# TensorE's order in the expert stage written out, Pool's residual passes one behind each scatter, expert weights ten chunks ahead

## The chip, the cores and the metric

One of the eight cores of a Trainium2 chip runs the kernel. The metric is the device time of one execution in microseconds (us). A core has five instruction streams that run side by side and wait for each other by semaphores: TensorE (PE in the profile; PEld is its weight load), VectorE (DVE), ScalarE (ACT), GpSimd (POOL) and SyncE (SP), which here only starts DMAs. Each stream runs strictly in its own order.

## The reference

One step of a backbone with two layers, model width 1024, for 128 context and 256 latent tokens, all fp32. A layer is a token mixer and then a mixture of experts, each inside `x <- LayerNorm(ALPHA*x + gate*sublayer(x*(1+scale)+shift))`. The change lies in the experts:

```python
def hier_moe(h, rg_w, rg_b, re_w, re_b, w1, w3, w2):      # h: 384 tokens x 1024
    g_idx = jnp.argmax(t @ rg_w + rg_b, axis=-1)          # one of 4 groups
    e_sel = ...                                           # its 8 expert logits
    top_v, top_i = lax.top_k(e_sel, 2)                    # two of 8 experts
    top_w = jax.nn.softmax(top_v, axis=-1) * g_p
    gate = ...                                            # 384 x 32, two entries a row
    hid = silu(einsum('td,edf->tef', t, w1)) * einsum('td,edf->tef', t, w3)
    return einsum('tef,efd->td', hid * gate, w2)          # 32 experts, each 1024 -> 128 -> 1024
```

## The kernel before, in words

The first 400 us of a layer's 570 or so are the mixer, which the change does not touch. Then comes the expert stage (`experts`, L1290), which runs once a layer.

The 32 experts are taken as 8 quads of four. Every expert has 32 token slots, and two experts of each quad (`who`, found at run time) get a second block of 32. A token is brought to its slots by one-hot matmuls: `gather(J)` (L1308) makes `xT`, 256 columns, the slots of two quads (J = 0 to 3), or `xB`, the second blocks of four quads (J = 4, 5). It has four steps of 12 matmuls (L1319), each evacuated from a `tp` bank, of which there are two; its one-hot matrix `oh` comes from VectorE (L1282, L1283) and needs `sidj`. `gather0` (L1322) is the first one in a form of its own.

A quad q then has these pieces:

- up: four weight chunks of 1 MB. Of each, `up_first` (L1362) is 8 matmuls with the weights in place, `up_second` (L1372) 8 matmuls with the weights of the two experts that `who` names, copied out to `hv` first (two copies a chunk, two of three on VectorE at L1353, one of three on ScalarE; `hv` has two buffers).
- hidden: Silu on ScalarE, a product on VectorE (L1381, `hid`), transposes on TensorE (L1383, L1385), a copy on VectorE (L1388, `hidT`).
- down: 8 matmuls with the second weights (L1398), 8 more with copies of them (L1405), in two `sc` banks; ScalarE and VectorE evacuate them to `ys` (two buffers) and `ys2` (one buffer), and Pool scatters each to memory by an indirect DMA (L1410), 14 a layer before the last quad. The last quad's rows stay on the chip.

`slots` (L1239) places the scatters' addresses and gates. `affine` (L1502) finishes the residual `r` on Pool: for three row blocks a subtraction and scaling (L1506), a product with `lg` (L1508) and a sum with `lb` (L1509). Both loads of `g20` and `g21` (L1512) then reuse the memory of `lg` and `lb`. After the last quad's hidden, a branch (L1519) for tokens beyond 64 in an expert, not taken here, and then the scattered rows come back (`yy`, L1589) and are summed with the last quad's (L1496, L1498) for the second LayerNorm.

The weights come in one queue, SyncE's, in the order of the program: 32 up chunks (L328; six `raw` buffers and four `wx` buffers, four of every ten chunks in `wx`) and 16 loads of 1 MB for down (L338, w2, four buffers). `done` (L343) asks for the next chunk after each one used, six ahead (`NRAW`). The last four chunks are held behind the fourteenth w2 load (L326).

Each stream's order is worked out by a scheduler when the kernel is built, from what each instruction needs, except inside `manual_schedule`, where the stream keeps the program's order; `issue_after` puts an instruction behind a named one.

Of the kernel before, what the change touches and what calls it, by code (L numbers as in the profile page):

```python
# [14 lines left out]
ALU = mybir.AluOpType  # L15
# [7 lines left out]
NT = 3  # L23
# [3 lines left out]
NQUAD = 8  # L27
NHALF = 16
# [49 lines left out]
class Kern:  # L78
# [177 lines left out]


    NRAW = 6

    def start_stream(self):  # L260

        o = []
        for l in range(L):
            ada = [("a", l, g, kp) for g in (1, 2) for kp in range(4)]
            if l + 1 < L:
                ada += [("a", l + 1, 0, kp) for kp in range(4)]
            for n in range(NPIECE // 4):
                if l == 0 and n < 2:
                    o.append(("a", 0, 0, n))
                o.append(("w", l, n))  # L270
                if l == 0 and n == 1:
                    o += [("a", 0, 0, 2), ("a", 0, 0, 3)]
                if n >= 1 and ada:
                    o.append(ada.pop(0))
            o += [("e", l, j) for j in range(NHALF)]
        self.order = [(*k, h) for k in o for h in range(2)]
        self.pos = {k: i for i, k in enumerate(self.order)}
        self.loaded = {}
        self.nload = 0
        self.ndone = 0  # L280
        self.limit = self.pos["w", 1, 0, 0]
        self.last_load = None
        self.prepped = {}

    def first_dma(self, out, in_):
# [26 lines left out]
    def load_to(self, n):  # L312
        if self.first_loads:
            return
        while self.nload < min(n, self.limit):
            k = self.order[self.nload]
            if k[0] == "e" and k[2] % 5 >= 3:
                w = self.wx.tile([128, 2048], F32, tag="wx", name="w_x")
            else:
                w = self.rawp.tile([128, 2048], F32, tag="raw", name="w_raw")  # L320
            src = {"a": lambda: self.a["wada"][(k[1] * 3 + k[2]) * 4 + k[3], k[4]],
                   "w": lambda: self.a["wst"][k[1] * (NPIECE // 4) + k[2], k[3]],
                   "e": lambda: self.a["w13"][k[1] * NHALF + k[2], k[3]]}[k[0]]()
            if k[0] == "e" and k[2] >= NHALF - 2:
                with self.tc.issue_after(self.w2_ins[k[1], NHALF - 3].ins):
                    self.nc.sync.dma_start(w, src)  # L326
            else:
                self.last_load = self.nc.sync.dma_start(w, src)  # L328
            self.loaded[k] = w
            self.nload += 1  # L330

# [13 lines left out]
    def done(self):  # L345

        self.ndone += 1
        self.load_first()
        self.load_to(self.ndone + self.NRAW)

    def prep(self, l, n):
        if n >= NPIECE or (l, n) in self.prepped:
# [787 lines left out]
    def gates(self, lg):  # L1140
        nc, mo, pc, m8, e8 = self.nc, self.mo, self.pc, self.m8, self.e8
        S = lambda name, shape, dt=F32: mo.tile([128, *shape], dt, name=name)
        sid, N6 = self.sid, 2 * NT
        self.sidj = S("sidj", (8, N6))
        self.sidj_ins = nc.vector.scalar_tensor_tensor(self.sidj, self.con[:, C_I32:C_I32 + 8].unsqueeze(2).to_broadcast([128, 8, N6]),
                                       -256.0, sid.rearrange("p i c -> p (i c)").unsqueeze(1).to_broadcast([128, 8, N6]),
                                       op0=ALU.mult, op1=ALU.add)

        ex = S("ex", (NT, 6))
        nc.vector.tensor_tensor(ex[:, :, 0:4], lg[:, :, 0:4], m8[:, :, 0:1].to_broadcast([128, NT, 4]), op=ALU.subtract)  # L1150
        nc.vector.tensor_tensor(ex[:, :, 4:6], e8[:, :, 0:2], e8[:, :, 0:1].to_broadcast([128, NT, 2]), op=ALU.subtract)
        with self.tc.issue_after(self.evac_ins.ins):
            self.act(ex, ex, AF.Exp)
        self.act(S("dum", (1,)), ex[:, 0, 0:1], AF.Silu)
        se = S("se", (NT, 2))
        nc.vector.tensor_reduce(se[:, :, 0], ex[:, :, 0:4], axis=AX.X, op=ALU.add)
        nc.vector.tensor_reduce(se[:, :, 1], ex[:, :, 4:6], axis=AX.X, op=ALU.add)
        nc.vector.reciprocal(se, se)
        nc.vector.tensor_tensor(se[:, :, 0], se[:, :, 0], se[:, :, 1], op=ALU.mult)
        self.W = S("W", (NT, 2))  # L1160
        nc.vector.tensor_tensor(self.W, ex[:, :, 4:6], se[:, :, 0:1].to_broadcast([128, NT, 2]), op=ALU.mult)


    def second(self):
        nc, mo, V = self.nc, self.mo, self.nc.vector
        S = lambda name, shape, dt=F32: mo.tile([128, *shape], dt, name=name)
        N6 = 2 * NT
        cnt = self.pc[:, 96:128].rearrange("p (q e) -> p q e", e=4)
        full = S("full", (NQUAD, 4))
        V.tensor_scalar(full, cnt, float(CAP), None, op0=ALU.is_gt)  # L1170
# [119 lines left out]
    def experts(self, l):  # L1290
        nc, mo, ep, tc = self.nc, self.mo, self.ep, self.tc
        scat = []
        iota = self.con[:, C_I256:C_I256 + 256]
        ident4 = self.ident.rearrange("p (i z r) -> p i z r", i=2, z=2)
        engines = [nc.vector.engine, nc.scalar.engine]
# [12 lines left out]
        def gather(J):  # L1308

            oh = self.onehot(J)  # L1310
            xT = slot_rows(J)
            for z in range(4):
                ps = self.bank("tp")
                for d2 in range(2):
                    d = z * 2 + d2
                    n = 0
                    for i in range(NT):
                        for t in (self.thi, self.tlo):
                            nc.tensor.matmul(ps[:, d2 * 256:(d2 + 1) * 256], t[:, i, d * 128:(d + 1) * 128], oh[:, i, :],  # L1319
                                             start=n == 0, stop=n == 5)  # L1320
                            n += 1
                evac(xT, z, ps)  # L1322
            return xT

        def gather0(oh):

# [49 lines left out]
        def hidden(ps):  # L1376
# [2 lines left out]
            hid = ep.tile([128, 3, 64], F32, tag="hid", name="hid", bufs=1)  # L1379
            self.act(hid, pv[:, :, 0, :], AF.Silu)  # L1380
            nc.vector.tensor_tensor(hid, hid, pv[:, :, 1, :], op=ALU.mult)  # L1381
            pt = self.bank("ms")
            nc.tensor.transpose(pt[:, 0:128], hid[:, 0:2, :].rearrange("p h f -> p (h f)"), self.ident)  # L1383
            for h in range(2):
# [24 lines left out]
        def scatter(view, rows, dst, n):  # L1409
# [3 lines left out]
            for o in scat:  # L1413
                tc.declare_no_dep(ins.ins, o.ins, reason="rows of other slots")
            scat.append(ins)

        def down(q, hT, who):
            ys = ep.tile([128, D], F32, tag="ys", name="ys", bufs=2)
# [14 lines left out]
        def down_keep(q, hT, who):  # L1433
# [11 lines left out]
                self.lo_ins = nc.vector.scalar_tensor_tensor(lo, src, g, hi.bitcast(F32), op0=ALU.mult, op1=ALU.subtract)  # L1445
            return ys, y2

        self.load_w2(l, 3)
        xT = gather0(self.oh0)
        self.gates(self.logit)  # L1450
        with tc.issue_after(self.oh0_ins.ins):
            self.second()
        _, who = nc.values_load_multi_w_load_instructions(
            self.who[0:1].rearrange("p q i -> p (q i)"), engines=engines, min_val=0, max_val=3,
            skip_runtime_bounds_check_because="a place among four, worked out as one")
        who = [who[2 * q:2 * q + 2] for q in range(NQUAD)]
        self.slots()
        xB = gather(4)
        for q in range(NQUAD - 1):
            ps = self.bank("mm")  # L1460
            for kq in range(4):
                up_first(ps, q, kq, xT)
                up_second(ps, q, kq, xB, who[q])
            hT = hidden(ps)
            if q % 2 == 0:
                nx = gather(q // 2 + 1) if q < 6 else None
            else:
                xT = nx
            if q == 3:
                xB = gather(5)  # L1470
            down(q, hT, who[q])
            if q == 0:
                self.affine(l, scat[0])
        q = NQUAD - 1
        ps = self.bank("mm")
        for kq in range(4):
            up_first(ps, q, kq, xT)
            up_second(ps, q, kq, xB, who[q])
        hT = hidden(ps)
        self.overflow(l)  # L1480
        self.load_yy(l)

# [17 lines left out]

    def affine(self, l, scat):

        nc, a, md = self.nc, self.a, self.m_d[l]
        with self.tc.issue_after(scat.ins):
            for i in range(NT):
                nc.gpsimd.tensor_scalar(self.r[:, i, :], self.r[:, i, :], self.nmean[:, i:i + 1], self.rs1[:, i:i + 1],  # L1506
                                        op0=ALU.add, op1=ALU.mult)
                nc.gpsimd.tensor_tensor(self.r[:, i, :], self.r[:, i, :], self.rows["lg"], op=ALU.mult)  # L1508
                nc.gpsimd.tensor_tensor(self.r[:, i, :], self.r[:, i, :], self.rows["lb"], op=ALU.add)  # L1509
        for s in range(2):  # L1510
            t = self.mo.tile([128, D], F32, tag="row", name=f"g2{s}", bufs=2)
            nc.sync.dma_start(t, md[1, s:s + 1, 1024:2048].to_broadcast([128, D]))  # L1512
            self.rows[f"g2{s}"] = t


    def overflow(self, l):
# [368 lines left out]
```

## Time and profile before

| | us |
|---|---|
| median of 3 runs | 1181.82 (1181.38 to 1182.83) |
| the profiled execution | 1179.99 |
| its span, first to last instruction | 1178.2 |
| TensorE's busy time in it | 1050.0 (89%) |
| VectorE's busy time | 835.5 (71%) |
| Pool's busy time | 284.2 (24%) |
| mean granted TensorE clock | 0.946 |

The expert stage of layer 0 runs from about 425 to 600 us of the span, that of layer 1 from about 995 us to the end. A row of a timeline gives when an instruction (or several of one kind, xN) started, how long it took, and in brackets how long its engine stood idle before it and what released it. The granted clock is a share of full speed.

### The profile page before, as it was taken

The page shows a single profiled execution, that of the slowest core. Times are in us where ns is not written, and L with a number is a line of the kernel's source. Part 1 is how long each engine was busy: PE and PEld are TensorE (multiplying, and loading weights), DVE is VectorE, ACT ScalarE, POOL GpSimd, SP SyncE. Part 2 cuts the span into 40 slices and gives each one's busy share as a digit, 9 for nine tenths or more (in the row PEclk, how much of TensorE's full clock was granted, in tenths as well). Part 3 has the DMA queues.
Part 4 walks back from the last instruction along what each step waited for, and adds up shares of the span by engine and source line. Part 5 has one row for each costly group of instructions (what it writes and reads, how often), then busy time and mean ns, then how long its engine had stood idle before and what let it go on. Part 6 is the DMA issues. An engine that isn't in the chain of part 4 may idle for free. (4 is left out here: it accounts for less than half of the span.)

```text
span 1178.2 us, 21160 instructions
## 1 busy us (share of the span) xinstructions
PE 1050.0 (89%) x8446; PEld 881.1 (75%) x8446; DVE 835.5 (71%) x1542; ACT 401.5 (34%) x687; POOL 284.2 (24%) x238
## 2 busy tenths in 40 slices
PE   7999999999999859598789999999999996859864
PEld 5898968878999848365359897788899996636532
DVE  3389999964458794754379999987634778684537
ACT  3334344453334121132253334435433422212222
POOL 0002411321101530611244043123110054061015
PEclk8999989999999968798889999999999998879997
DMA  9967568357366544599595756772233675468964
GB/s 356 400 235 269 208 241 316 119 192 273 110 232 255 185 175 165 219 398 418 234 345 173 272 206 248 268 274 100 77 139 111 248 269 202 152 237 330 419 255 158
DMA packets 53950, 279.37 MB, mean 237 GB/s; under 512 B 7932, under 2 KB 12028, under 8 KB 26705
## 3 DMA queue, kind: packets, MB, share of 16 engines
q1 hardware_dynamic: 49344, 269.75, 60.4%
q0 software_dynamic: 4496, 8.14, 1.9%
q8 instruction: 71, 1.16, 0.4%
q14 instruction: 39, 0.31, 0.1%
HBM read 261.86 MB, written 21.56 MB: 241 GB/s over the span
## 5 line engine op out<-in xcount | busy, mean ns | idle before, releaser
L95 PE MATMUL ps_mm<-hThi,wr 128*128 128x384 f32 x672 | 230.3, 344 | 5.3 <-ACT hThi L100 2.9
L108 DVE TENSOR_TENSOR wr<-w_raw,wr 128x1024 fp32r<-128x1024 f32 x124 | 163.0, 1315 | 95.9 <-ACT wr L100 95.6
L97 PE MATMUL ps_mm<-hThi,wr 128*128 128x384 f32 x672 | 228.0, 339 | 1.3 <-DVE wr L108 1.3
L96 PE MATMUL ps_mm<-hTlo,wr 128*128 128x384 f32 x672 | 228.1, 339 | 0.4 <-DVE hTlo L437 0.2
L100 ACT ACTIVATE wr<-w_raw 128x1024 fp32r<-128x1024 f32 x140 | 147.3, 1055 | 68.7 <-PE ps_mm L97 36.4
L501 DVE SCALAR_TENSOR_TENSOR cacc<-pad,par,cacc 128x399 f32<-128x399 f32 x240 | 167.4, 698 | 4.1
L95 PEld LDWEIGHTS ps_mm<-hThi,wr 128*128 128x128 f32 x672 | 127.2, 189 | 21.8 <-ACT hThi L100 5.2
L97 PEld LDWEIGHTS ps_mm<-hThi,wr 128*128 128x128 f32 x672 | 127.3, 189 | 3.6 <-DVE wr L108 1.6
L96 PEld LDWEIGHTS ps_mm<-hTlo,wr 128*128 128x128 f32 x672 | 127.2, 189 | 2.8 <-DVE hTlo L437 1.3
L1410 POOL DMA_INDIRECT y_d<-ys,dst x28 | 28.5, 1019 | 238.3 <-ACT hv L100 89.5
L1372 PE MATMUL ps_mm<-hv,xB 128*32 128x128 f32 x1024 | 51.1, 280 | 29.3 <-DVE hv L1353 28.7
L108 POOL TENSOR_TENSOR wr<-w_raw,wr 128x1024 fp32r<-128x1024 f32 x10 | 24.8, 2478 | 207.8 <-ACT wr L100 207.3
L1372 PEld LDWEIGHTS ps_mm<-hv,xB 128*32 128x32 f32 x1024 | 36.3, 111 | 42.7 <-DVE hv L1353 35.7
L1319 PE MATMUL ps_tp<-oh,thi 128*128 128x256 f32 x240 | 66.7, 311 | 1.6 <-DVE xB L1302 1.6
L1319 PE MATMUL ps_tp<-oh,tlo 128*128 128x256 f32 x240 | 64.0, 300 | 0.0
L1353 DVE COPY hv<-w_x 128x512 f32 x36 | 47.6, 1367 | 17.4 <-PE ps_mm L1372 9.9
L1319 PEld LDWEIGHTS ps_tp<-oh,thi 128*128 128x128 f32 x240 | 50.0, 209 | 11.3 <-issue 4.9
L1319 PEld LDWEIGHTS ps_tp<-oh,tlo 128*128 128x128 f32 x240 | 49.9, 208 | 1.2 <-issue 1.0
L1398 PE MATMUL ps_sc<-w,hidT 128*32 128x512 f32 x256 | 36.2, 670 | 16.2 <-PEq L1519 8.4
L100 ACT ACTIVATE gate<-ps_mm 128x384 f32<-128x384 f32 x40 | 19.7, 491 | 85.7 <-PE ps_mm L97 84.7
L211 PE MATMUL ps_ms<-w_raw,cT 128*32 128x512 f32 x320 | 47.3, 621 | 0.0
L1362 PE MATMUL ps_mm<-w_raw,xT 128*32 128x256 f32 x640 | 47.1, 385 | 0.0
(491 smaller groups left out, 2383.0 us busy)
## 6 DMA issues: line engine op xcount, KB each, us to landing
w_raw<-in_wst SPq DMA_DIRECT2D x68, 1024.0 KB, 6.5
w_raw<-in_wada SPq DMA_DIRECT2D x48, 1024.0 KB, 5.2
w_raw<-in_w SPq DMA_DIRECT2D x40, 1024.0 KB, 9.0
w<-in_w SPq DMA_DIRECT2D x32, 1024.0 KB, 10.3
w_x<-in_w SPq DMA_DIRECT2D x24, 1024.0 KB, 9.4
bias<-in_bias SPq DMA_DIRECT2D x8, 768.0 KB, 8.7
y_d<-zero SPq DMA_DIRECT2D x2, 3072.0 KB, 15.7
yy<-y_d SPq DMA_DIRECT2D x6, 1024.0 KB, 8.1
```

Source lines behind the costliest of these rows:

```text
L95: mm(out, whi, xhi, start=first, stop=False)
L96: mm(out, whi, xlo, start=False, stop=False)
L97: mm(out, wlo, xhi, start=False, stop=last)
L100: return self.nc.scalar.activation(out, in_, f, **k)
L108: (eng or self.nc.vector).tensor_tensor(lo, x, hi.bitcast(F32), op=ALU.subtract)
L211: nc.tensor.matmul(ps[32 * t:32 * t + 32, :], self.cT[:, 2 * kp + k, :], w[:, t * 512:t * 512 + 512], start=(kp == 0 and k == 0), stop=(kp ...
L501: nc.vector.scalar_tensor_tensor(acc, pad[:, j:j + W], w, acc, op0=ALU.mult, op1=ALU.add)
L1319: nc.tensor.matmul(ps[:, d2 * 256:(d2 + 1) * 256], t[:, i, d * 128:(d + 1) * 128], oh[:, i, :], start=n == 0, stop=n == 5)
L1353: nc.vector.tensor_copy(hv[:, i, :], src)
L1362: nc.tensor.matmul(ps[e * 32:(e + 1) * 32, 0:256], xT[:, k, c:c + 32], w[:, e, kk, :], start=k == 0, stop=k == 7, skip_group_check=True)
L1372: nc.tensor.matmul(ps[t * 32:(t + 1) * 32, 256:384], xB[:, k, c:c + 32], hv[:, i, kk, h * 128:(h + 1) * 128], start=False, stop=k == 7, sk ...
L1398: nc.tensor.matmul(po[e * 32:(e + 1) * 32, :], hT[:, e * 32:(e + 1) * 32], w2[:, e, :], start=True, stop=True)
```

## The change

Three things, all in the expert stage.

The order of TensorE's instructions there is that of the program. The program now gives: `gather0`, then `up_first` of quads 0 and 1 (64 matmuls), `gather(4)`, `up_second` and hidden of quad 0, `slots`; then for each quad the up, the down of the quad before it, the transposes of hidden (`hidden_T`), and half of a gather. `sidj` is made in `second` with the columns that are used, four and two.

`affine` is a generator that is advanced by each scatter: one Pool pass behind each of the first nine. The two loads that reuse the memory of `lg` and `lb` come in the program with the tenth scatter.

`done` asks for chunks ten ahead in this stage, and the first ten are asked for at its start; the four last chunks are no longer held behind a w2 load.

```diff
+    ahead = NRAW
...
-            if k[0] == "e" and k[2] >= NHALF - 2:
-                with self.tc.issue_after(self.w2_ins[k[1], NHALF - 3].ins):
-                    self.nc.sync.dma_start(w, src)
-            else:
-                self.last_load = self.nc.sync.dma_start(w, src)
+            self.nc.sync.dma_start(w, src)
...
-        self.load_to(self.ndone + self.NRAW)
+        self.load_to(self.ndone + self.ahead)
...
+            next(aff, None)
...
-        xB = gather(4)
-        for q in range(NQUAD - 1):
-            ps = self.bank("mm")
-            for kq in range(4):
-                up_first(ps, q, kq, xT)
-                up_second(ps, q, kq, xB, who[q])
-            hT = hidden(ps)
-            if q % 2 == 0:
-                nx = gather(q // 2 + 1) if q < 6 else None
...
-            down(q, hT, who[q])
-            if q == 0:
-                self.affine(l, scat[0])
+        self.ahead = self.NRAW + 4
+        self.load_to(self.ndone + self.ahead)
+        with tc.manual_schedule(engines={nc.tensor.engine}):
+            xT = gather0(self.oh0)
...
+            gb = gather(4)
+            xB = next(gb)
+            self.gates(self.logit)
+            pss = [self.bank("mm") for _ in range(2)]
+            for q in range(2):
+                for kq in range(4):
+                    up_first(pss[q], q, kq, xT)
+            self.run(gb)
             for kq in range(4):
...
+                up_second(pss[0], 0, kq, xB, who[0])
+            hid = hidden(pss[0])
+            self.slots()
...
+                    hid = hidden(ps)
+                    if q == 3:
+                        self.run(g)
+                        gb = gather(5)
+                        xB = next(gb)
+                        self.run(gb)
+                    down(q - 1, hT.pop(q - 1), who[q - 1])
+                hT[q] = hidden_T(hid)
+                if g is not None:
+                    for _ in range(2):
+                        next(g, None)
...
+            for k in range(3):
+                with self.tc.issue_after(scat[-1].ins):
+                    if k == 0:
+                        nc.gpsimd.tensor_scalar(r, r, self.nmean[:, i:i + 1], self.rs1[:, i:i + 1], op0=ALU.add, op1=ALU.mult)
+                    else:
+                        nc.gpsimd.tensor_tensor(r, r, rows["lg" if k == 1 else "lb"], op=ALU.mult if k == 1 else ALU.add)
+                yield
```

TensorE's stream at the start of layer 0's expert stage, before: the end of `gather0` (oh, tlo), two chunks of `up_first`, `slots`, and `gather(4)`.

```order
L1331 MATMUL ps_tp<-oh,tlo 128x256 x2
L1331 MATMUL ps_sc<-oh,tlo 128x256 x2
L1362 MATMUL ps_mm<-w_raw,xT 32x256 x16
L1239 MATMUL ps_ms<-V,RO 128x96 x12
L1319 MATMUL ps_tp<-oh,thi 128x256
```

The same place after the change (lines 1327, 1358 and 1315 are what 1331, 1362 and 1319 were).

```order
L1327 MATMUL ps_tp<-oh,tlo 128x256 x2
L1327 MATMUL ps_sc<-oh,tlo 128x256 x2
L1358 MATMUL ps_mm<-w_raw,xT 32x256 x48
L1358 MATMUL ps_mm<-w_x,xT 32x256 x16
L1315 MATMUL ps_tp<-oh,thi 128x256
```

Six more chunks of `up_first` stand between `gather0` and the next gather, and `slots` has gone behind `up_second` of quad 0. Further on in TensorE's stream, quad 2 after the change: its up (1358, 1368), the down of quad 1 (1397, 1404), and only then the transposes of quad 2's hidden (1382, 1384).

```order
L1358 MATMUL ps_mm<-w_raw,xT 32x256 x8
L1368 MATMUL ps_mm<-hv,xB 32x128 x8
L1397 MATMUL ps_sc<-w_3740,hidT 32x512 x4
L1397 MATMUL ps_sc<-w_4065,hidT 32x512 x4
L1404 MATMUL ps_sc<-hv,hidT 32x256 x8
L1382 MATMUL ps_ms<-con,hid 128x128
L1384 MATMUL ps_ms<-con,hid 64x64 x2
```

Before, the transposes of a quad stood directly behind its up, and its own down soon behind them.

Pool's stream in the same stage, before: the passes on `r` behind the first two scatters (each DMA is a scatter).

```order
L1508 TENSOR_TENSOR r_3476<-r_3476,lg 128x1024 x3
L1509 TENSOR_TENSOR r_3476<-r_3476,lb 128x1024 x3
L1410 DMA y_d<-ys,dst 768x1024
L1410 DMA y_d<-ys_4664,dst 1536x512
L1410 DMA y_d<-ys,dst 768x1024
```

After the change (1409 is what 1410 was, 1528 is 1506, 1530 is 1508 and 1509), from the second pass to the sixth.

```order
L1530 TENSOR_TENSOR r_3476<-r_3476,lg 128x1024
L1409 DMA y_d<-ys,dst 768x1024
L1530 TENSOR_TENSOR r_3476<-r_3476,lb 128x1024
L1409 DMA y_d<-ys_4760,dst 1536x512
L1528 TENSOR_SCALAR r_3476<-r_3476,nmean,rs_3875 128x1024
L1409 DMA y_d<-ys,dst 768x1024
L1530 TENSOR_TENSOR r_3476<-r_3476,lg 128x1024
L1409 DMA y_d<-ys_5016,dst 1536x512
L1530 TENSOR_TENSOR r_3476<-r_3476,lb 128x1024
```

The passes stand one by one between scatters; only the last two stand together. SyncE's queue near the end of the stage, before: the last chunks (326), and the last two w2 loads.

```order
L338 DMA w_5263<-in_w 128x2048
L338 DMA w_5265<-in_w 128x2048
L326 DMA w_x<-in_w 128x2048 x2
L326 DMA w_raw<-in_w 128x2048 x2
L338 DMA w_5397<-in_w 128x2048
L338 DMA w_5399<-in_w 128x2048
```

After the change (324 and 334 are what 328 and 338 were; 1534 loads `g20` and `g21`).

```order
L324 DMA w_raw<-in_w 128x2048 x2
L334 DMA w_5329<-in_w 128x2048
L334 DMA w_5331<-in_w 128x2048
L1534 DMA g_5325<-m_d_110 128x1024
L1534 DMA g_5327<-m_d_110 128x1024
L334 DMA w_5483<-in_w 128x2048
L334 DMA w_5485<-in_w 128x2048
```

The loads of `g20` and `g21`, which before went out in the stage's first half, now stand ahead of the last two w2 loads.

## Rows read from the trace of the kernel before

**Rows 1.** Waits of TensorE, 425 to 579 us: us in total, times, longest.
```profile
PE ps_mm L1372 <- DVE hv L1353: 14.5, 4, 13.5
PE ps_ms L1239 <- DVE V L1235: 5.8, 1, 5.8
PE ps_sc L1398 <- PEq L1519: 4.2, 1, 4.2
PE ps_ms L1383 <- DVE hid L1381: 3.6, 4, 1.1
PE ps_sc L1398 <- DVE hidT L1388: 2.3, 3, 1.4
```

**Rows 2.** Windows of layer 0: PE, PEld, DVE, ACT, POOL busy, clock, DMA share, GB/s.
```profile
440.30:448.00 7.70, 7.70 (x36) 7.70 (x37) 4.84 (x30) 0.60 (x1) 0.00 (x0) 0.51 0.18 74
...
489.00:496.00 7.00, 6.50 (x61) 5.18 (x65) 3.72 (x11) 1.45 (x3) 0.00 (x0) 0.77 0.61 225
```

**Rows 3.** Timeline of VectorE around the long wait, layer 0.
```profile
471.22 17.77 DVE L1353 COPY hv<-w_x 128x512 f32 x3 [2.16 <-PE ps_mm L1372]
```

**Rows 4.** The copies from `w_x` in layer 0: ns min/median/max, first and last start.
```profile
L1353 DVE COPY hv<-w_x x18: 409/428/14780, 471.2 to 568.0; 128x512 f32 x18
```

**Rows 5.** Timeline of Pool around the same wait.
```profile
470.11 3.54 POOL L1506 TENSOR_SCALAR r<-r,nmean,rs 128x1024 f32<-128x1024 f32 x3
473.82 1.02 POOL L1410 DMA_INDIRECT y_d<-ys,dst  x1 [0.17 <-issue]
474.88 6.94 POOL L1508 TENSOR_TENSOR r<-r,lg 128x1024 f32<-128x1024 f32 x3
481.78 6.92 POOL L1509 TENSOR_TENSOR r<-r,lb 128x1024 f32<-128x1024 f32 x3
```

**Rows 6.** The longest wait of TensorE in layer 1, 1001 to 1146 us.
```profile
PE ps_mm L1372 <- DVE hv L1353: 14.2, 3, 13.5
```

**Rows 7.** Timeline of TensorE, quad 0's down, a gather and quad 1's up.
```profile
465.50 1.04 PE L1398 MATMUL ps_sc<-w,hidT 128*32 128x512 f32 x8
466.50 1.07 PE L1405 MATMUL ps_sc<-hv,hidT 128*32 128x256 f32 x16
...
467.72 0.28 PE L1319 MATMUL ps_tp<-oh,tlo 128*128 128x256 f32 x1
...
470.30 0.28 PE L1319 MATMUL ps_tp<-oh,tlo 128*128 128x256 f32 x1
...
470.97 1.05 PE L1362 MATMUL ps_mm<-w_raw,xT 128*32 128x256 f32 x16
471.83 0.62 PE L1372 MATMUL ps_mm<-hv,xB 128*32 128x128 f32 x16
472.27 1.05 PE L1362 MATMUL ps_mm<-w_x,xT 128*32 128x256 f32 x16
```

**Rows 8.** Timeline of SyncE: the eleventh chunk, and the queue during the long wait.
```profile
437.54 18.62 SPq L328 DMA_DIRECT2D w_raw<-in_w  x4
...
474.08 15.30 SPq L328 DMA_DIRECT2D w_x<-in_w  x2
...
549.51 3.12 SPq L338 DMA_DIRECT2D w<-in_w  x2
```

**Rows 9.** DMA from 500 to 570 us, with the w2 loads' size, count and landing.
```profile
DMA packets 4712, 27.62 MB, mean 395 GB/s; under 512 B 996, under 2 KB 996, under 8 KB 1698
...
w<-in_w SPq DMA_DIRECT2D x8, 1024.0 KB, 15.8
```

**Rows 10.** The end of layer 0's quads on ScalarE.
```profile
573.49 0.69 ACT L100 ACTIVATE ys<-ps_sc,gate 128x512 f32<-128x512 f32 x1 [0.45 <-DMA y_d<-ys,dst]
```

**Rows 11.** The last scatter before the branch, on Pool.
```profile
574.45 0.98 POOL L1410 DMA_INDIRECT y_d<-ys,dst  x1 [2.99 <-ACTq L1519]
```

**Rows 12.** The tile `y_d`, layer 0: issue to landing of its DMAs.
```profile
DMA to landing us min/median/max: 2.9/8.2/11.2
```

**Rows 13.** From the page's costliest groups: Pool's passes of this size in the mixer.
```profile
L108 POOL TENSOR_TENSOR wr<-w_raw,wr 128x1024 fp32r<-128x1024 f32 x10 | 24.8, 2478 | 207.8 <-ACT wr L100 207.3
```

## What the change is expected to do

> **What bounds the kernel now.** I read the list of TensorE's waits over the expert stage first, because TensorE is the busiest engine and the change writes down its order; then the timelines of the engines named in the longest waits; then SyncE and the DMA view, which say whether a faster TensorE would find its weights there.
>
> The reader is to see three things. First, TensorE loses 14.5 us in layer 0 to `hv` copies, 13.5 of them in one wait, and layer 1 has the same wait [rows 1, 6]. VectorE's row explains it: three copies that began at 471.22 took 17.77 us [rows 3], one of them 14.78 where the median is 0.43 [rows 4]. Pool's row beside it shows what ran meanwhile: six passes on `r`, back to back, from 474.88 to 488.70 [rows 5]. So while Pool works on SBUF in this form, a copy of VectorE that is already issued does not finish. Second, before `slots` TensorE waits 5.8 us for `V`, the end of a chain of small VectorE instructions, and comes out of it at half clock: 0.51 granted over the next 7.7 us [rows 1, 2]; after the long wait the clock is 0.77 over 7 us. Third, smaller waits for hidden, 3.6 and 2.3 us, and 4.2 us for the branch, which stays as it is [rows 1].
>
> DMA is next in line: from 500 to 570 us it moves 395 GB/s [rows 9], and no view of this kernel shows much more. The last w2 loads are issued from 549.51 over 3.12 us [rows 8] and take some 15.8 us [rows 9], so they land at about 568, not long before they are used.
>
> **The sum, per layer, against the profiled execution (1179.99).**
>
> *The long wait goes.* With one pass between two scatters no train of six stands before a copy: -13.5. The clock after it: 7.0 us at 0.77 would be 7.0 x 0.23 = 1.6 shorter at full speed, so -1.6 [rows 2].
>
> *What the spread passes give back.* The nine passes are still there: 3.54 + 6.94 + 6.92 = 17.4 us of Pool [rows 5]. Bounds: 0, if each falls beside matmuls that have their copies already, and 17.4, if TensorE waits out each of them. Now a pass that follows the scatter of `ys` runs beside transposes and half a gather. A gather matmul comes every (470.30 - 467.72)/22 = 0.117 us [rows 7], so 24 of them are 2.8 us, longer than a pass of 2.3. That cover holds while a gather is left. A pass behind the scatter of `ys2` falls on the copies of the next up, where two buffers of `hv` give TensorE a lead of one chunk: 471.83 - 470.97 = 0.86 plus about 0.44 for the second part, 1.3 us [rows 7]. It loses 2.3 - 1.3 = 1 us. Four or five of the nine stand so; I take +4.
>
> By the row a copy waited out a whole train, 14.78 us, not one instruction. The Trainium skill, page "SBUF — State Buffer", section "Who interferes with whom", says that VectorE's fp32 copies and GpSimd share a port pair that goes to the one that issues first "for the whole instruction", the other blocking fully. By that rule the copy could have come in after one pass of 2.3 us, and the trace does not agree: it had to wait for six. The rule also says that a single spread pass still blocks a copy entirely, which is rival A. By the trace a train is what is dear, and the change breaks the train.
>
> *The gap before `slots`.* Six more chunks of `up_first` now stand where TensorE waited 5.8 us. They are 6 x 0.86 = 5.2 us of work that before came later [rows 7], and their ten buffers were filled early (the eleventh chunk goes out at 437.54, when the first buffer is freed [rows 8]): -5.2. Without the gap the clock does not fall: 7.7 us at 0.51 hold 7.7 x 0.49 = 3.8 us [rows 2]. `gather(4)` may still wait a little for its one-hot matrix, so I take -3.0 of it, with 0 and -3.8 as bounds.
>
> *Waits for hidden.* The down of the quad before, 1.00 + 1.00 + 1.00 us [rows 7], now stands between a quad's up and its transposes, and half a gather between the transposes and the down. That covers waits of 1 us each [rows 1]. Of 3.6 + 2.3 I take -4.0: one of each is left at the end, where nothing follows.
>
> *The tail.* The sum so far is for TensorE. What ends the stage is the last scatter's landing, which the rows' return needs. `ys2` has one buffer: its next evacuation waits for the scatter of the last one to land. Each step of that chain is an evacuation of 0.69 [rows 10], a scatter of 0.98 [rows 11], and 2.9 to 11.2 us of landing [rows 12]. Before, TensorE was slow enough that the chain was hardly waited for (0.45 us at 573.49 [rows 10]). With quads coming faster it is waited for, and each down now comes one quad later, so the seventh's comes directly before the end. Bounds: 0, and 8 if two more steps of median length stick out under the 4.2 us of the branch; I take +4.
>
> *At nothing.* The ten-deep look-ahead: SyncE's queue already holds the next chunk at each buffer's release [rows 8], and buffers, not requests, set the time. It moves w2 loads later in the queue; the 15.3 us in which SyncE stood still during the long wait [rows 8] are then free for loads. If that cover is gone, a w2 load is late by at most its landing. `g20` and `g21` now wait for the eighth and ninth pass, which free their memory, and the last two w2 loads stand behind them in SyncE's queue. Those are used only after the branch, so up to 15.8 - 4.2 = 11.6 us are at stake if the ninth pass runs as late as the last transposes; it follows the ninth scatter of 14, so I cost it at nothing. `sidj` in six columns saves or costs 0.1 us at most beside the matmuls.
>
> Sum: -13.5 - 1.6 + 4 - 5.2 - 3.0 - 4.0 + 4 = -19.3 us a layer, -38.6 for two. The profiled execution would be 1141.4. It lies 1.8 below the median of the runs, so 1143.
>
> **Rivals.**
>
> A. *Each pass still takes a copy with it, and every copy is late.* Nine passes cost 17.4 less the covers of the four or five that stand before a gather, about 10, and the chain of `ys2` costs its 8. Then -13.5 - 1.6 - 8.2 - 4 + 10 + 8 = -9.3, times two: about 1163; with the whole 17.4 it is 1178. For it: the rows show no copy that ran through a two-input pass. Against: the other two copies of the three took 17.77 - 14.78 = 3.0 us together, and they began beside the scalings at 470.11 [rows 3 to 5]. It is also what the rule of the Trainium skill above ("SBUF — State Buffer") makes of single passes. Chance 0.18.
>
> B. *All fits and the loads are the limit.* After 437.54 there are 22 chunks, 12 w2 loads, the two rows and the scatters to move, some 40 MB; at 395 GB/s [rows 9] that is 101 us, so the last load lands at about 540 and not 568. TensorE's own work from 432.5 on is 8 ups of 5.2, 7 downs of 3.0, five gathers of 5.6, and 6 for transposes and `slots`, 97 us, ready by 530. The gain is then 27 us a layer, 1128 in all. For it: all waits named are covered on paper. Against: the passes and `ys2` have to cost nothing. Chance 0.16.
>
> C. *Slower: a pass in Pool's queue holds the scatters.* A scatter now stands behind a pass. If a pass waits for VectorE as long as VectorE's copies go on, the scatter behind it waits too, `ys` and `ys2` are not freed, ScalarE stops at the next evacuation with the `hv` copies behind it, and TensorE, whose order is now fixed, can't pass on to other work. A quad's copies are strung along its up, 4 x 1.30 = 5.2 us [rows 7]; nine waits of most of that, 4.5 us, are 40 in place of my +4, and the layer comes out at -23.3 + 40 = +17: 1215. It decides from 23.3/9 = 2.6 us a pass on. Against it: in the mixer ten passes of this size took 2.48 us in the mean [rows 13], 2.3 beside the copies here, so Pool has not been seen to wait. Chance 0.05.
>
> D. *Late weights at the end.* The ninth pass comes late, because the `ys2` chain holds the ninth scatter, and the last w2 loads come up to 11.6 us late. A gain of 8 to 14 us a layer is left, 1154 to 1166. For it: SyncE's queue is in order. Against: the ninth scatter belongs to quad 3 or 4. Chance 0.12.
>
> **How the numbers follow.** My forecast, 1143 with 1133 to 1152 as its own range, has 0.45; A 0.18, B 0.16, D 0.12, C 0.05, and 0.04 are for what I don't see. The ends of the unknown terms alone give: all good, -13.5 - 1.6 - 5.2 - 3.8 - 5.9 = -30 a layer, held to -27 by the loads; all bad, +17.4 and +8, -2 a layer. The range goes from 1122 to 1170: it takes in B whole, D, and A but for its far end. A difference of 0.2% (2.4 us) is about what a measurement of this kernel can tell from no change. Faster than that: 0.92; within it: 0.03, A's far end; slower: 0.05, C.
>
> **What would show it.** In the profile of the changed kernel the long wait of `up_second` for `hv` must be gone in both layers, and no copy of VectorE longer than about 3 us. Waits of 1 us each for `hv` must stand beside single passes; if they are over 2 us at most passes, A is right. `slots` must have no wait and the granted clock must stay near 1 from 432 to 450. ScalarE's evacuation of `ys2` should wait for DMAs in the last quads, and the last scatter should follow the last transposes by more than the branch. If TensorE's first w2 matmuls after the branch wait for a DMA, D is right; if Pool's passes take longer than 2.5 us, C. I am wrong at the root if TensorE shows new waits at the pieces moved, above all at the down of the quad before.

## The result, and the profile after

The changed kernel takes 1149.63 us (median of 4 runs, 1144.31 to 1156.94) where the kernel before takes 1182.32 beside it: a ratio of 0.9722, interval 0.9665 to 0.9780. In another set of runs (e5 below) it was 1147.62 against 1180.79, 0.9717 (0.9670 to 0.9764). Forecast were 1143 and, as a range, 1122 to 1170. The profiled execution took 1144.31, the fastest of the four.

TensorE's waits in the expert stage of layer 0 (425 to 570 us): us in total, times, longest. They answer to [rows 1].

```profile
PE ps_mm L1368 <- DVE hv L1349: 5.8, 5, 2.1
PE ps_tp L1315 <- DVE oh L1277: 4.0, 2, 2.3
...
PE ps_sc L1404 <- DVE ys L1424: 2.6, 3, 0.9
PE ps_sc L1397 <- ACT ys L100: 2.4, 3, 0.8
```

The wait of 13.5 us and the wait before `slots` are gone, and so are those for hidden. New is the wait for the one-hot matrix, and the waits for `ys` at the down rose from 3.4 to 5.0 us.

TensorE's part of the stage, from the first `up_first` to the last transposes, as windows: first of the kernel before (layer 0, layer 1), then of the changed one. The columns are length, PE, PEld, DVE, ACT, POOL busy, granted clock, DMA share, GB/s.

```profile
432.50:573.80 141.30, 110.68 (x1537) 76.58 (x1536) 80.40 (x190) 33.09 (x59) 30.68 (x22) 0.89 0.71 282
1002.20:1141.20 139.00, 107.69 (x1537) 74.22 (x1536) 80.63 (x190) 33.13 (x59) 31.04 (x23) 0.91 0.72 285
```

```profile
430.90:548.10 117.20, 101.50 (x1536) 70.39 (x1535) 72.31 (x188) 32.68 (x58) 29.92 (x21) 1.00 0.84 337
980.60:1099.90 119.30, 102.20 (x1537) 70.32 (x1536) 72.47 (x188) 32.62 (x58) 29.74 (x21) 1.00 0.82 329
```

Of the 24.1 us that layer 0 gains here, idle time (length less PE busy) is 30.6 - 15.7 = 14.9 and busy time 9.2: the same matmuls, at a granted clock that is 1.00 all along where it was 0.89. Of the 19.7 us of layer 1, idle time is 14.2 and busy time 5.5.

Not all of it reaches the end. SyncE sends for the scattered rows at 579.11 before and at 557.75 after; from the first `up_first` that is 146.6 and 126.8 us, a gain of 19.8, and in layer 1 141.9 and 127.8, a gain of 14.1. ScalarE and Pool show where the rest is lost (changed kernel, end of layer 0):

```profile
545.68 0.69 ACT L100 ACTIVATE ys<-ps_sc,gate 128x512 f32<-128x512 f32 x1 [0.56 <-DMA y_d<-ys,dst]
553.22 0.69 ACT L100 ACTIVATE ys<-ps_sc,gate 128x512 f32<-128x512 f32 x1 [6.85 <-DMA y_d<-ys,dst]
```

```profile
549.07 1.12 POOL L1409 DMA_INDIRECT y_d<-ys,dst  x1 [0.31 <-issue]
554.18 0.97 POOL L1409 DMA_INDIRECT y_d<-ys,dst  x1 [3.98 <-ACTq L1541]
```

ScalarE stands idle for 6.85 us before it evacuates the last `ys2`, whose matmuls ended at 548.2, 5 us earlier: it waits for the landing of the scatter that began at 549.07 and still reads the one buffer. Where [rows 11] had the last scatter right behind the last transposes, it now starts 6 us after they do.

### The profile page after: what moved, and what is told of

It is laid out like the page before. It is cut to its first block, busy times and chain, and to the rows that moved or that the text cites. A ratio compares the mean times of both kernels' runs of the same rounds, so it can differ in the third digit from the quotient of the medians.

```text
span 1142.5 us, 21165 instructions
## 1 busy us (share of the span) xinstructions
PE 1037.9 (91%) x8446; PEld 870.9 (76%) x8446; DVE 825.6 (72%) x1542; ACT 401.3 (35%) x687; POOL 286.3 (25%) x238
## 5 line engine op out<-in xcount | busy, mean ns | idle before, releaser
L108 DVE TENSOR_TENSOR wr<-w_raw,wr 128x1024 fp32r<-128x1024 f32 x124 | 165.5, 1335 | 95.0 <-ACT wr L100 94.7
L96 PEld LDWEIGHTS ps_mm<-hTlo,wr 128*128 128x128 f32 x672 | 127.0, 189 | 3.1 <-DVE hTlo L433 1.7
L1315 PE MATMUL ps_tp<-oh,thi 128*128 128x256 f32 x240 | 59.8, 289 | 7.6 <-DVE oh L1277 7.6
L1315 PE MATMUL ps_tp<-oh,tlo 128*128 128x256 f32 x240 | 57.7, 280 | 0.0
L1368 PE MATMUL ps_mm<-hv,xB 128*32 128x128 f32 x1024 | 44.9, 275 | 13.3 <-DVE hv L1349 11.6
L1315 PEld LDWEIGHTS ps_tp<-oh,thi 128*128 128x128 f32 x240 | 45.2, 188 | 10.2 <-issue 9.0
L1368 PEld LDWEIGHTS ps_mm<-hv,xB 128*32 128x32 f32 x1024 | 32.5, 109 | 26.1 <-DVE hv L1349 15.8
L1315 PEld LDWEIGHTS ps_tp<-oh,tlo 128*128 128x128 f32 x240 | 45.2, 188 | 0.1
L1358 PE MATMUL ps_mm<-w_raw,xT 128*32 128x256 f32 x640 | 41.0, 380 | 0.3 <-DVE xT L1297 0.2
L903 POOL TENSOR_TENSOR rtmp<-sc,lb 128x1024 f32<-128x1024 f32 x4 | 10.0, 2510 | 121.6 <-DVE st L944 60.9
```

The source lines that it names most:

```text
L96: mm(out, whi, xlo, start=False, stop=False)
L108: (eng or self.nc.vector).tensor_tensor(lo, x, hi.bitcast(F32), op=ALU.subtract)
L1358: nc.tensor.matmul(ps[e * 32:(e + 1) * 32, 0:256], xT[:, k, c:c + 32], w[:, e, kk, :], start=k == 0, stop=k == 7, skip_group_check=True)
L1368: nc.tensor.matmul(ps[t * 32:(t + 1) * 32, 256:384], xB[:, k, c:c + 32], hv[:, i, kk, h * 128:(h + 1) * 128], start=False, stop=k == 7, sk ...
```

## The experiments

Each is read by the same spans: from the first `up_first` to the last transposes, and to the load of the scattered rows; us, layer 0 and layer 1 of the profiled execution. In the code below `...` marks lines left out.

| kernel | median (before beside it) | to the transposes | to the load of rows |
|---|---|---|---|
| before | 1182.32 | 141.3, 139.0 | 146.6, 141.9 |
| after | 1149.63 (1182.32) | 117.2, 119.3 | 126.8, 127.8 |
| e1 passes spread only | 1173.43 (1177.47) | 137.6, 133.6 | 142.9, 141.5 |
| e2 after, passes together | 1169.53 (1177.47) | 131.9, 130.6 | 141.5, 139.2 |
| e3 after, no passes | (layer 0 only) | 113.0 | 122.3 |
| e4 after, two `ys2` | 1123.59 (1177.47) | 113.6, 111.3 | 119.6, 116.6 |
| e5 after again | 1147.62 (1180.79) | 117.9, 120.6 | 127.0, 128.5 |
| e6 e4 with covered passes | 1118.78 (1180.79) | 106.5, 107.0 | 115.1, 115.5 |
| e7 before, two `ys2` | 1173.62 (1180.79) | 136.9, 136.1 | 140.0, 138.6 |
| e8 after, old start | 1158.98 (1180.79) | 125.5, 124.4 | 135.0, 132.5 |
| e9 e6, `g` rows last | 1115.83 (1178.51) | 107.0, 106.0 | 116.3, 113.8 |
| e10 e6 again | 1114.64 (1178.51) | 108.4, 104.9 | 116.6, 113.0 |

**e1, the spread passes alone, and e2, all but them.** e1 is the kernel before with the new `affine`, advanced in `scatter`:

```diff
+            next(aff, None)
...
-            if q == 0:
-                self.affine(l, scat[0])
```

> The kernel before with one thing of the change: one Pool pass behind each of the first nine scatters, TensorE's order left to the scheduler, loads as before. Theory 1 (the train of six passes made the long wait): the 13.5 us wait for hv goes in both layers, some 5 us of hv waits of 1 to 2 us each come in its place, the wait before slots stays at 5.8 us; about 10 us a layer less, near 1162 us. Theory 2 (the wait went because TensorE's new order gives it other work): the long wait or its sum in pieces stays, over 10 us of hv waits a layer, 1175 to 1182 us.

e2 is the reverse, the kernel after with `affine` run at once behind quad 0's down:

```diff
-            next(aff, None)
...
+                    if q == 1:
+                        self.run(self.affine(l, scat[:1]))
```

> The kernel after with the nine passes put back behind the first scatter as in the kernel before, in trains; all else as after. Theory 1 (the train): a wait for hv of over 10 us comes back in each layer, since TensorE's written order has no other work ahead of it; near 1165 to 1172 us. Theory 2 (the order covers it): waits for hv stay near 6 us a layer and the time near 1150.

The waits of TensorE for `hv` in layer 0, first e1, then e2:

```profile
PE ps_mm L1373 <- DVE hv L1354: 6.6, 7, 2.1
```

```profile
PE ps_mm L1367 <- DVE hv L1348: 12.5, 2, 12.4
```

So the train makes the long wait: it goes when the passes are spread and comes back when they are not. In e2 the instruction that the train holds, to 0.3 us behind the pass that ends at 480.22, is not a copy but one for the one-hot matrix, and the copies that TensorE waits for stand behind it:

```profile
467.96 12.55 DVE L1277 SCALAR_TENSOR_TENSOR oh<-con,sidj,oh 128x256 fp32r<-128x256 f32 x1
```

But e1 gained only 3.7 us of TensorE in layer 0 (5.4 in layer 1) where I had said 10, and its ratio is 0.995 (0.9923 to 0.9976). Its idle time in layer 0 fell by 6.8 us, since shorter waits came up behind (those for `hidT` went from 2.3 to 4.4 us), and its busy time rose by 3.1, since the clock still fell while TensorE worked. (The mean of a window counts idle stretches too: the kernel before had 0.50 from 480 to 490 us, with TensorE busy for 0.96 us of the ten.) In the changed kernel the same edit is worth 131.9 - 117.2 = 14.7 us (11.3 in layer 1). Together the two parts gain more than apart: 24.1 us against 3.7 + 9.4.

The window of e1's stage in layer 0, for its clock:

```profile
431.00:568.60 137.60, 113.77 (x1537) 77.08 (x1536) 78.79 (x190) 32.59 (x59) 31.68 (x22) 0.91 0.74 290
```

**e3, what the single passes still cost.** The passes are not issued:

```diff
-                with self.tc.issue_after(scat[-1].ins):
-                    ...
                 yield
```

> The kernel after without the nine passes on r (this part of the computation is left out, so the residual isn't normalised). It prices what the single passes still cost. Theory 1: TensorE's waits for hv fall from 5.8 us a layer to under 1.5, and 4 to 5 us a layer of TensorE time go, of which the chain of ys2 at the end gives part back: 1138 to 1147 us. Theory 2 (each pass blocks more than its row shows, rival A): 10 us or more a layer go, under 1130.

Without them the second layer gets other numbers, and the branch for tokens beyond 64 in an expert is taken; the whole takes 1793 us. Layer 0 is unchanged up to there, and it is all that is read. Of the waits for `hv` from VectorE, 5.8 us in the changed kernel, 0.2 are left, and TensorE's part is 117.2 - 113.0 = 4.2 us shorter. In the changed kernel's own rows one sees which passes cost. Pool and VectorE during the up of quad 4, before which no gather stands:

```profile
499.27 2.38 POOL L1530 TENSOR_TENSOR r<-r,lg 128x1024 f32<-128x1024 f32 x1
501.81 1.03 POOL L1409 DMA_INDIRECT y_d<-ys,dst  x1 [0.17 <-issue]
502.87 2.35 POOL L1530 TENSOR_TENSOR r<-r,lb 128x1024 f32<-128x1024 f32 x1
```

```profile
499.57 5.95 DVE L1349 COPY hv<-w_x 128x512 f32 x3 [0.94 <-PE ps_mm L1368]
505.44 1.24 DVE L1349 COPY hv<-w 128x512 f32 x3
```

Three copies take 5.95 us. The first starts behind the first pass's start and ends 0.3 us behind its end. The third starts at 502.19, before the second pass, and still ends 0.3 us behind that one:

```profile
502.19 3.32 DVE L1349 COPY hv<-w_x 128x512 f32 x1
```

TensorE waits 0.79 and 2.07 us there, the second its longest wait for `hv`. The Trainium skill ("SBUF — State Buffer", "Who interferes with whom") has a two-port instruction of VectorE and one of GpSimd share a port pair: whichever issues first holds it for the whole instruction, and the other fully blocks. The first copy agrees with that. The third does not, by its start, nor does the copy of 14.78 us in [rows 4], which started at 488.99 - 14.78 = 474.21, before the train's first pass at 474.88 [rows 3, 5].

Passes hold other work of VectorE too. During the up of quad 2:

```profile
464.53 2.39 POOL L1530 TENSOR_TENSOR r<-r,lg 128x1024 f32<-128x1024 f32 x1
```

```profile
464.43 3.18 DVE L1276 TENSOR_SCALAR oh<-con,sidj 128x256 fp32r<-128x256 f32 x3
```

Three such instructions for the one-hot matrix take 0.87 us at 494.64, with no pass beside them. The copies stand behind them here, and TensorE waits 1.60 us for `hv`; a wait of 1.18 us at 531.06 comes about in the same way.

**e4, two buffers for `ys2`, and e7, the same in the kernel before.**

```diff
-                    y2 = ep.tile([128, 512], F32, tag="ys2", name="ys2", bufs=1)
+                    y2 = ep.tile([128, 512], F32, tag="ys2", name="ys2", bufs=2)
```

(Room comes from `sl`, which shares the buffers of `hidT`, and a tile of the router that moves to a pool closed earlier.)

> The kernel after with two buffers for ys2 in place of one; room for it comes from a small tile moved to another pool and one that shares a buffer. Theory 1 (the single buffer makes the tail): ScalarE's evacuations of ys2 no longer wait for a landing, from the last transposes to the load of the scattered rows it is about 5 us and not 9, and the sc bank that ys2 held for a quad is free, which takes up to 5 us a layer of waits for ys off TensorE: 1130 to 1142 us. Theory 2 (the last scatter's own way sets the end): the same time as after within 3 us, 1147 to 1152.

> The kernel before with two buffers for ys2 and nothing else. Theory 1 (the one buffer came to matter only when TensorE's order drew the quads together): at most the waits for ys, 3.4 us a layer, go; 1170 to 1178 us where the kernel before takes 1177. Theory 2 (it was a limit all along, and the change only left it): 20 us or more less.

e4 takes 0.9511 of the time before (0.9462 to 0.9560) where the changed kernel takes 0.9722: some 25 us less, more than I expected. The end is shorter, and TensorE's part too, by 3.6 and 8.0 us: with one buffer an unread result stood in one of two `sc` banks for a quad, and the last three downs waited for `ys`. Those waits, 5.0 us in the changed kernel's layer 0, are gone from e4's list. Its last two scatters, Pool, layer 0:

```profile
548.02 0.96 POOL L1409 DMA_INDIRECT y_d<-ys,dst  x1 [6.97 <-issue]
549.29 0.98 POOL L1409 DMA_INDIRECT y_d<-ys,dst  x1 [0.30 <-DVE hv L1349]
```

They stand 1.3 us apart, not 5. In the kernel before the second buffer gives 0.9945 (0.9922 to 0.9968), and takes 1.2 and 2.4 us of TensorE's idle time where in the changed kernel it takes 5.5 and 7.9: the one buffer came to matter when the quads were drawn together.

**e8, the start of the stage as before.**

```diff
-            for q in range(2):
-                for kq in range(4):
-                    up_first(pss[q], q, kq, xT)
+            for kq in range(2):
+                up_first(pss[0], 0, kq, xT)
+            self.slots()
             self.run(gb)
+            for n in range(2, 8):
+                up_first(pss[n // 4], n // 4, n % 4, xT)
...
-            self.slots()
```

> The kernel after with the start of the stage as before: two chunks of up_first, slots, gather(4), and only then the six other chunks. Theory 1 (the six chunks fill the wait for V): a wait of 5 to 6 us before slots comes back, with TensorE at half clock after it; 5 to 8 us more a layer, 10 to 16 in all. Theory 2 (the order there is free, since VectorE's chain sets the time anyway): the same as after within 3 us.

```profile
PE ps_ms L1233 <- DVE V L1229: 5.5, 1, 5.5
```

The wait is back, and TensorE's part is 8.3 and 5.1 us longer than in the changed kernel's first profile, 7.6 and 3.8 longer than in e5's, which ran beside it (1158.98 against 1147.62).

**e5, the changed kernel again.**

> The kernel after, once more, beside the others of this call, so that they can be compared on one chip; and to see whether its runs lie as far apart again (1144 to 1157). Both theories: near 1147, with a spread of some 10 us if it comes from where the scatters' landings fall in the ys2 chain (theory 1), or of 2 to 3 us if the first spread was of the chip (theory 2).

Its runs lay 9 us apart again, those of e4 and e6 some 5. That would fit the chain of landings, but the kernel before spread as far; and of the 3.3 us between the two profiled executions of the changed kernel 2.6 had come about before layer 0's expert stage began. The cause of the spread stays open.

**e6, passes where a gather follows; e9 and e10.** Two `ys2` buffers, other places for the passes, and the down of quad 2 ahead of `gather(5)`:

```diff
+        for p in ((0, 0), (1, 0), (0, 1), (2, 0), (0, 2), (1, 1), (1, 2), None, (2, 1), (2, 2)):
...
                     if q == 3:
                         self.run(g)
+                    down(q - 1, hT.pop(q - 1), who[q - 1])
+                    if q == 3:
                         gb = gather(5)
...
-                    down(q - 1, hT.pop(q - 1), who[q - 1])
```

> The kernel after with two buffers for ys2, the down of quad 2 moved ahead of gather(5), and the Pool passes placed where a gather follows: one behind each of the first seven scatters (the three scalings behind the first, second and fourth), none behind the eighth, one behind the ninth and the tenth. Theory 1 (a pass costs only where no gather stands behind its scatter): waits for hv fall from 4.6 us a layer to 1 to 2, the second wait for the one-hot matrix (2.3 us) goes, TensorE's stage is 4 to 6 us shorter a layer than with two ys2 buffers alone, if the loads allow it: 1110 to 1117 us beside 1123.6. Theory 2 (the loads are now the limit, or the passes cost the same wherever they stand): within 3 us of 1123.

Waits for `hv` fell to 2.4 us a layer, where I had said 1 to 2, and TensorE's part by 7.1 and 4.3 us against e4; what each of the two moves gave of that was not measured. The whole takes 0.9476 of before (0.9443 to 0.9509), an interval that overlaps e4's. From the last transposes to the load of the rows it is 8.6 us again, and half of the gain is lost there: to the load it is 4.5 and 1.1. Was that the loads? In e9 the loads of `g20` and `g21` stand behind the last two w2 loads.

> The kernel of e6 (two ys2 buffers, passes where a gather follows, quad 2's down ahead of gather(5)) with the loads of g20 and g21 behind the last two w2 loads. Theory 1 (the end of the stage is now set by the loads: in e6 the last w2 load landed 6 us after the last transposes, and the last scatters shared the queue with it): 1 MB less ahead of them at some 400 GB/s is 2.5 us a layer; 3 to 6 us less than e6 in all. Theory 2 (the scatters' landing alone sets the end): the same as e6 within 2 us.

> The kernel of e6 once more, for a comparison with e9 on one chip: 1116 to 1121 by both theories.

Their order did not matter: e9 and e10 are the same within their runs. In e9 the last w2 load landed at 543.4, 5 us before the last scatters did, and still the load of rows came 9.3 us behind the last transposes. What sets it is the way of the last two scatters from issue to landing, in layer 0 of e9 and of e4:

```profile
DMA to landing us min/median/max: 6.6/7.1/7.7
DMA to landing us min/median/max: 3.2/3.6/4.0
```

Why it is twice as long in e9 is open. The loads are not ruled out: in e9 those of `g20` and `g21` landed at 546.3 and 547.5, beside these scatters, and the DMA share was 0.57 from 543 to 545, where beside e4's it was 0.25 to 0.41.

**The look-ahead** needed no run: built with six chunks ahead in place of ten, all five streams hold the same instructions in the same order. The last four chunks, no longer held behind a w2 load, and the smaller `sidj` have no run of their own.

## Why the prediction was right, step by step

The long wait: as forecast; e2 brings 12.4 us of it back. The passes: +4 forecast, 4.2 measured (e3), and in part for the reason given: no gather stood behind the scatter. The prediction reckoned with `hv` copies alone; of the four waits behind passes, two (1.60 and 1.18 us) came from other work of VectorE that a pass held. The gap: -8.2 forecast with the clock, 8.3 and 5.1 by e8; part went into a new wait of 1.8 us for the one-hot matrix of `gather(4)`. Hidden: -4.0 forecast, and all 5.9 went. At nothing: the look-ahead changed no order. `g20` and `g21` did wait for Pool, 8.6 us in SyncE's list, but no TensorE wait for a w2 load followed; rival D fell.

Two terms were mis-sized. The clock: I took 1.6 + 3.0 from two windows, and busy time fell by 9.2 in layer 0, because the clock fell in a third stretch too, behind waits of 0.5 to 0.9 us, and 10 x 0.34 = 3.4 us were lost there (kernel before, columns as above):

```profile
550.00:560.00 10.00, 8.87 (x126) 5.62 (x130) 3.77 (x9) 1.46 (x3) 1.00 (x1) 0.66 1.01 419
```

Of those waits the ones for hidden went with the change; the ones for `ys` are still there, and the clock stays at 1.00.

The idle time: the terms for waits (-13.5 + 4 - 5.2 - 4.0) make -18.7, and it fell by 14.9. Missing in the sum were most of the 4.0 us of waits for the one-hot matrix, 2.3 of them at `gather(5)`, and the 1.6 us by which the waits for `ys` grew. The last paragraph of the prediction had named new waits at the pieces moved as a sign of being wrong at the root; they came, but did not outweigh the gain.

The tail: +4 forecast, +4.3 and +5.6 between transposes and load of rows; its place and cause were right, but I saw only the end of the chain. That the unread `ys2` also held a bank, at 3.6 and 8.0 us of TensorE a layer (e4), was in no step.

The sum was -19.3 a layer and came out at -19.8 and -14.1. That layer 0 came so near is luck in part: 4.6 us too little for the clock and 3.8 too much for the waits cancel. Layer 1 gave 5.7 less than layer 0, whose rows I doubled. Of that, 3.7 is busy time: before the change layer 1 had lost less to the clock (PE busy 107.7 against 110.7 us). Another 0.7 is idle time, and 1.3 the end, which before stood 2.9 us behind the transposes and not 5.3.

Of the rivals, A fell with e3. But one argument against it was misread. The 3.0 us of two copies beside the scalings [rows 3 to 5] were no sign that copies run beside them: one of the two took 2.72 us, to 0.3 us behind the last scaling, and the other 0.42. B's 1128 was not the floor of the loads: e10 is at 1114.64. C fell: none of Pool's passes took over 2.41 us, against 2.3 in [rows 5].

## What to carry to other kernels

A train of Pool passes held an instruction of VectorE to the train's end, a copy for 14.78 us and in e2 one for the one-hot matrix for 12.55; put single passes where TensorE needs nothing from VectorE for as long as a pass takes, copies or other. What an order written by hand gains is decided by the clock too, here 9.2 of 24.1 and 5.5 of 19.7 us, so count busy time at both clocks. After such a change look at once for single buffers whose release is a DMA's landing: here the second buffer gave some 25 us where the change gave 33.

## What the hardware showed that was not expected

Removing waits one by one gained 3.7 (e1) where the same removal in the tight order gained 14.7 us: behind gaps of 1.10, 2.07 and 0.79 us between 500 and 508 e1's clock fell to half (granted 0.58 from 508 to 512), behind 0.79 and 2.07 the changed kernel's did not (granted 1.00 from 500 to 510). In e1 a gather followed, in the changed kernel a down. What decided it these runs don't show.
